# Scan steps traced between single projection tiles, decays split into four steps

## The chip, the core and the metric

The kernel runs on one core of a Trainium2 chip. The metric is the device time of one execution in microseconds (us); the median of three runs of the kernel before is 1252.73 us. Five engines work side by side, each through its own queue of instructions in order: TensorE (PE in the profile; its weight loads are PEld), VectorE (DVE), ScalarE (ACT), GpSimd (POOL) and SyncE (SP), which here only issues transfers.

## The reference, cut to what matters

One layer of a diffusion backbone on 512 latent tokens and 256 context tokens of width 1024. One input projection (`w_in`) feeds a convolution branch and a state-space mixer that scans in both directions; both are gated, merged, projected, and an MLP follows. The change touches the mixer and the convolution branch's first half (GLU and taps):

```python
glu = proj[..., COL_GLU:COL_GATE]
u = glu[..., :CONV_DIM] * jax.nn.sigmoid(glu[..., CONV_DIM:])
u = dwconv(u.reshape(bsz * n_seg, seg_len, CONV_DIM), ...)       # 31 taps
...
xbc = jax.nn.silu(dwconv(proj[..., COL_XBC:COL_DT], ...))        # x, B, C: 5 taps
# the scan, per direction, in chunks of 128 tokens
decay = jnp.exp(jnp.where(lower, seg, -jnp.inf))                 # seg[q,k] = cum[q] - cum[k]
cb = jnp.einsum('bcqgn,bckgn->bcgqk', cs_, bs)
y_diag = jnp.einsum('bcgrqk,bckgrp->bcqgrp', cb[:, :, :, None] * decay, xdt)
states = jnp.einsum('bcqgn,bcqgr,bcqgrp->bcgrpn', bs, decay_to_end, xdt)
y_off = jnp.einsum('bcqgn,bcgrpn,bcqgr->bcqgrp', cs_, h_in, jnp.exp(cum))
y = y_f + flip(y_b) + D * x;  y = rmsnorm(y * silu(z))
```

There are 32 heads in 8 groups of 4; a group shares B and C.

## The kernel before

Activations lie transposed, 128 channels on the partitions and 512 tokens along the row. Every matrix product of a projection is made of three fp32r products (high by high, high by low, low by high). `load_w` (L104) loads a raw weight tile of 128x1024 (two buffers), rounds it on ScalarE to `whi` (L110), and subtracts on VectorE to get `wlo` (L111); `gemm` (L114) then runs 24 matmuls of 512 columns into one of three PSUM buffers `ps`.

The kernel opens with the adaLN modulation and the first projections, then runs the mixer over 8 groups (about 107 to 605 us of the profile), then the rest of the GLU tiles, gates, output projections and the MLP.

A group g needs six projection tiles, made by `proj` (L425): B, C, X0 and X1 through `xbc` (L384), which also does the 5 taps on VectorE (L381) and a SiLU on ScalarE (L391), B and the two X with 256 context columns besides; and Z0, Z1 with a SiLU (L440). The scan of a group is `ssd` (L471):

- `cps` = B by C per chunk (L476), copied to `cb` (L478); transposes of B to `bps` (L484), copied to `Bk` (L485).
- transposes of X to `xps` (L495), scaled on VectorE to `xw` (L500) and copied on ScalarE to `xt` (L507).
- the state of each chunk, `sps` (L515), the first copied on ScalarE to `hst` (L521), the others added up on VectorE (L527, L528).
- for each half j of two heads: four rows of exp(cum) are broadcast from DRAM to `Cd` (L537) and multiplied by C on GpSimd or VectorE (L538); the decays `M` of the two heads are multiplied by `cb` (L541); 32 matmuls with the states (L555) and 16 with `xt` (L551; the profile's counts) fill `yps`; then `yt` (L559, L560), which goes to DRAM, and its square (L566), which GpSimd adds up (L567).

The decays come from `expo` (L450). For each head and each of two directions it broadcasts a row of cum from DRAM to a tile `E` (L459), masks it on GpSimd (L463), takes the exponential on ScalarE in four pieces (L466), and adds the two directions on VectorE (L468). Before the loop it is traced for four heads; then each half y of a group traces the next two heads, all four steps in a row. The forward tiles have 7 buffers, the backward ones 3.

`glu` (L570) makes one of 8 GLU tiles from two projection tiles, with a Tanh (L576) between, and `taps` (L584) its 31-tap convolution on VectorE (30 instructions at L594). Five of the eight are traced inside the group loop, one at the end of groups 0 to 4. The order of tracing per group is thus: whole scan of g, all six projection tiles of g+1, a GLU tile and its taps.

That order is not the order in which engines run. A planner lays out each engine's queue when the kernel is built: an instruction's priority is its place in the tracing, moved by `later(n)`; among those that it takes to be ready at a moment of its own simulated time, the first in priority goes next. Weight loads are moved 300 places ahead (`W_EARLY`), evictions 400 (`EVICT`), taps 650 back (`TAPS_LATER`). What the planner lays out is fixed; on the chip each engine takes its queue in order.

Of the kernel before, what the change touches and what calls it, by code (L numbers as in the profile page):

```python
# [20 lines left out]
G = 8  # L21
# [8 lines left out]
CDB, EB, LEAD, ADDV, E_LATER, E_LATER0 = 7, 7, 2, 1, 0, 0  # L30
# [18 lines left out]
GLU_AT = tuple(range(5))  # L49
# [12 lines left out]
def build(tc, xT, ctxT, cond, crow, wada1, wada2, vecs, hv, cst, w_in, w_co, w_so, w_o, w_1, w_2, outT):  # L62
    nc = tc.nc
    with ExitStack() as es:
# [49 lines left out]
        def gemm(ps, w, rhs, start=True, stop=True, t0=0, t1=None, k0=0, k1=KT):  # L114
            whi, wlo = w
            rhi, rlo = rhs
            ps = ps[:, t0:t1]
            for k in range(k0, k1):
                nc.tensor.matmul(ps, lhsT=whi[:, k, :], rhs=rhi[:, k, t0:t1], start=start and k == 0, stop=False)  # L119
                nc.tensor.matmul(ps, lhsT=whi[:, k, :], rhs=rlo[:, k, t0:t1], start=False, stop=False)  # L120
                nc.tensor.matmul(ps, lhsT=wlo[:, k, :], rhs=rhi[:, k, t0:t1], start=False, stop=stop and k == KT - 1)  # L121

        psum_pools = [pp]
        turn = [0]
# [300 lines left out]
        def proj(g):  # L425
            s = W_GRP + 6 * g
            if g == 0:
                _, Bt, Ct, X = first_xbc
            else:
                Bt = xbc(s, 16 + g, True, "Bt")  # L430
                Ct = xbc(s + 1, 24 + g, False, "Ct")
                X = [xbc(s + 2 + j, 2 * g + j, True, "Xt") for j in range(2)]
            Z = []
            for j in range(2):
# [6 lines left out]
                Z.append(z)  # L441
            return Bt, Ct, X, Z
# [4 lines left out]
        ahead = []  # L447
        asked = [0]

        def expo(upto):  # L450

            while asked[0] < min(upto, HEADS):
                h = asked[0]
                asked[0] += 1
                es_ = []
                for d in range(2):
                    hd = d * HEADS + h
                    e = (tp if d else spool).tile([P, T], F32, name="E", tag="M" if d else "E", bufs=3 if d else EB)
                    nc.sync.dma_start(e, s_cf[hd, 0].unsqueeze(0).broadcast_to([P, T]))  # L459

                    x3 = e.rearrange("p (c q) -> p c q", q=P)
                    sign = -1 if d else 1
                    nc.gpsimd.affine_select(x3, x3, pattern=[[0, NCH], [sign, P]], compare_op=ALU.is_ge,  # L463
                                            fill=never, base=0, channel_multiplier=-sign)
                    for c in range(NCH):
                        nc.scalar.activation(x3[:, c], x3[:, c], AF.Exp, bias=bT[:, c, hd:hd + 1])  # L466
                    es_.append(e)
                (nc.vector if ADDV else nc.gpsimd).tensor_tensor(es_[0], es_[0], es_[1], ALU.add)  # L468
                ahead.append(es_[0])

        def ssd(g, Bt, Ct, X, Z):  # L471
            ch = lambda t, c: t[:, c * P:(c + 1) * P]

            cps = pm.tile([P, T], F32, name="cps", tag="pm")
            for c in range(NCH):
                nc.tensor.matmul(ch(cps, c), lhsT=ch(Bt, c), rhs=ch(Ct, c), start=True, stop=True)  # L476
# [4 lines left out]
            for c0, n in ((0, 4), (4, 2)):  # L481
                pt = pm.tile([P, T], F32, name="bps", tag="pm")
                for c in range(n):
                    nc.tensor.transpose(ch(pt, c), ch(Bt, c0 + c), ident)  # L484
                nc.scalar.copy(Bk[:, c0 * P:(c0 + n) * P], pt[:, :n * P])  # L485

            xt = spool.tile([P, NCH, 4, 64], F32, name="xt", tag="xt", bufs=1)
            xw = [spool.tile([P, 5, 4, 64], F32, name=f"xw{d}", tag=f"xw{d}", bufs=1) for d in range(2)]
            wi = [lambda c: c if c < 3 else c - 1, lambda c: c - 1]
            hs = lambda d: slice(d * HEADS + 4 * g, d * HEADS + 4 * g + 4)  # L490
            for c0 in (4, 0, 2):
                pt = pm.tile([P, T], F32, name="xps", tag="pm")
                for c in range(2):
                    for j in range(2):
                        nc.tensor.transpose(  # L495
                            pt[:, c * 256 + j * P:c * 256 + (j + 1) * P], ch(X[j], c0 + c), ident)
# [5 lines left out]
                for d in range(2):  # L502
                    lo = c0 + 1 if (d == 1 and c0 == 0) else c0
                    hi = c0 + 1 if (d == 0 and c0 == 2) else c0 + 2
                    scaled(xw[d][:, wi[d](lo):wi[d](hi - 1) + 1], ptv[:, lo - c0:hi - c0], wgT[:, lo:hi, hs(d)])
                if c0 < 4:
                    nc.scalar.copy(xt[:, c0:c0 + 2], ptv)  # L507

            hst = spool.tile([P, NCH, 2, 256], F32, name="hst", tag="hst", bufs=1)

            def states(chunks):
                ps = pm.tile([P, T], F32, name="sps", tag="pm")
                for d in range(2):
                    for i, c in enumerate(chunks[d]):
                        nc.tensor.matmul(  # L515
                            ps[:, d * 256:(d + 1) * 256], lhsT=ch(Bk, c),
                            rhs=xw[d][:, wi[d](c)].rearrange("p h e -> p (h e)"),
                            start=i == 0, stop=i == len(chunks[d]) - 1)
# [3 lines left out]
            for s in range(NCH - 1):  # L522
# [5 lines left out]
                nc.vector.tensor_tensor(nxt, nxt, ps.rearrange("p (d h e) -> p d h e", d=2, h=4), ALU.add)  # L528

            for j in range(2):  # L530
                yps = py.tile([P, T], F32, name="yps", tag="py")
                Ms, Cs = [], ([], [])
                for r in range(2):
                    for d in range(2):
                        hd = d * HEADS + 4 * g + 2 * j + r
                        Cd = (spool if d else tp).tile([P, T], F32, name="Cd", tag="Cd", bufs=CDB if d else 3)
                        nc.sync.dma_start(Cd, s_cf[hd, 1].unsqueeze(0).broadcast_to([P, T]))  # L537
                        (nc.vector if (d, r) in DECAYS_V else nc.gpsimd).tensor_tensor(Cd, Ct, Cd, ALU.mult)  # L538
                        Cs[d].append(Cd)
                    M = ahead.pop(0)  # L540
                    nc.vector.tensor_tensor(M, M, cb, ALU.mult)  # L541
                    Ms.append(M)
                with later(E_LATER):
                    expo(4 * g + 2 * j + 2 + LEAD)
                for k in range(3):
                    for c in range(NCH):
                        for r in range(2):
                            o = yps[64 * r:64 * r + 64, c * P:(c + 1) * P]
                            hr = 2 * j + r
                            if k == 2:  # L550
                                nc.tensor.matmul(o, lhsT=xt[:, c, hr, :], rhs=ch(Ms[r], c),  # L551
                                                 start=False, stop=True, skip_group_check=True)
                            else:
                                s = 3 - c if k else c
                                nc.tensor.matmul(o, lhsT=hst[:, s, k, hr * 64:hr * 64 + 64], rhs=ch(Cs[k][r], c),  # L555
                                                 start=k == 0 and c == 0, stop=False, skip_group_check=True)
                t = 2 * g + j
                yt = tp.tile([P, T], F32, name="yt", tag="yt", bufs=2)
                nc.vector.scalar_tensor_tensor(yt, X[j][:, :T], vcol(V_D + t), yps, ALU.mult, ALU.add)  # L559
                nc.vector.tensor_tensor(yt, yt, Z[j], ALU.mult)  # L560
                nc.sync.dma_start(s_y[t], yt)
                if t == 0:
                    nc.scalar.activation(yacc, yt, AF.Square)
                else:
                    q = spool.tile([P, T], F32, name="ysq", tag="ysq", bufs=1)
                    nc.scalar.activation(q, yt, AF.Square)  # L566
                    nc.gpsimd.tensor_tensor(yacc, yacc, q, ALU.add)  # L567


        def glu(t, pool, tag):  # L570
# [4 lines left out]
            with later(-EVICT_GLU):  # L575
                nc.scalar.activation(sg, pb, AF.Tanh, scale=0.5)  # L576
            wa = load_w(w_in[W_GLU + 2 * t + 1])
# [37 lines left out]
        late = list(range(len(GLU_AT), KT))  # L615
# [28 lines left out]
        for t in late:  # L644
            q = glu(t, tp, "e")
# [251 lines left out]
```

## Times and profile before

| | |
|---|---|
| three runs | 1252.73, 1250.56, 1253.77 us (median 1252.73) |
| profiled execution | 1248.84 us, span of the program in it 1247.0 us |
| granted TensorE clock, mean | 0.993 |
| weight tiles through L110 | 163, mean 1049 ns |
| exponentials at L466 | 256 pieces, mean 393 ns |
| masks at L463 | 64, mean 979 ns |
| rows `E` and `Cd` | 64 transfers each of 256 KB, 4.9 and 4.8 us to landing |

The profile is of one execution. A waits view gives an engine's idle time by what ended it: total us, times, longest. A windows view gives each engine's busy time in a stretch, with the number of instructions that touch it. A timeline view gives start and length of merged instructions, and in brackets the idle time before them and what ended it. Ends of matmuls are modelled: back to back, they overlap in the trace, so a busy TensorE isn't one at its full pace. SP's waits for buffers cost nothing by themselves.

### The profile page before, as it was taken

What the parts mean: (1) busy time and instruction counts of PE and PEld (TensorE: products, weight loads), DVE (VectorE), ACT (ScalarE), POOL (GpSimd) and SP (SyncE); (2) the same over time, 40 slices, a digit from 0 to 9 for tenths busy, and PEclk for the clock granted to TensorE, in tenths of its full rate; (3) what the DMA queues carried; (4) which work ended last, traced back from release to release, by engine and by line L of the source; (5) the groups of instructions that cost most, each with busy time, mean ns of one, the idle gap of its engine ahead of it and who ended that gap; (6) DMA issues with size and microseconds to landing.
All of it is one profiled execution on the core that took longest, in us unless ns stands there. A gap on an engine that the chain in (4) does not pass through costs nothing.

```text
span 1247.0 us, 17404 instructions
## 1 busy us (share of the span) xinstructions
PE 1202.9 (96%) x6662; PEld 995.0 (80%) x6662; DVE 924.0 (74%) x1426; ACT 545.2 (44%) x900; POOL 173.4 (14%) x138
## 2 busy tenths in 40 slices
PE   6998999999999999999999999999999999999997
PEld 3787788787787887787888788788988888888886
DVE  6798799899998989776999698776833343443454
ACT  4557876455554445342452561234522332322342
POOL 0004444142242424120010000000000000000000
PEclk8999999999999999999999999999999999999998
DMA  9427573442535352322353468945112323322332
GB/s 366 142 68 225 163 228 103 125 150 93 178 93 178 110 162 78 118 71 91 123 180 119 134 198 289 308 150 166 54 41 96 101 90 97 102 93 94 101 101 68
DMA packets 65331, 169.83 MB, mean 136 GB/s; under 512 B 7648, under 2 KB 10464, under 8 KB 65120
## 3 DMA queue, kind: packets, MB, share of 16 engines
q1 hardware_dynamic: 65248, 168.72, 42.0%
q8 instruction: 52, 0.85, 0.3%
q14 instruction: 31, 0.25, 0.1%
HBM read 162.14 MB, written 6.55 MB: 135 GB/s over the span
## 4 chain that ended last, share of the span: by engine, by line
PE 59%; DVE 21%; DMA 10%; ACT 4%; issue 3%; POOL 1%; SPq 0%; DVEq 0%; ACTq 0%; POOLq 0%
PE ps L119 18%; PE ps L121 18%; PE ps L120 17%; DVE conv L594 7%; DVE wlo L111 3%; PE sps L515 3%; DMA Cd<-s_cf 3%; DVE Xt L381 3%; DMA aw<-in_wada_dram 2%; PE yps L555 1%; DMA E<-s_cf 1%; DVE Ct L381 1%; DMA yr<-s_y 1%; DVE Bt L381 1%; POOL E L463 1%
## 5 line engine op out<-in xcount | busy, mean ns | idle before, releaser
L110 ACT CAST whi<-raw 128x1024 fp32r<-128x1024 f32 x163 | 170.9, 1049 | 363.6 <-PE ps L120 332.5
L111 DVE TENSOR_TENSOR wlo<-raw,whi 128x1024 fp32r<-128x1024 f32 x163 | 203.5, 1249 | 98.3 <-ACT whi L110 86.8
L121 PE MATMUL ps<-hh,wlo 128*128 128x512 f32 x632 | 254.6, 403 | 3.8 <-DVE wlo L111 3.6
L119 PE MATMUL ps<-hh,whi 128*128 128x512 f32 x632 | 255.2, 404 | 2.5 <-DVE Bt L381 1.7
L120 PE MATMUL ps<-hl,whi 128*128 128x512 f32 x632 | 253.7, 401 | 0.0
L594 DVE SCALAR_TENSOR_TENSOR conv<-sg,V,conv 128x392 f32<-128x392 f32 (+14 forms) x240 | 181.7, 774 | 1.8
L121 PEld LDWEIGHTS ps<-hh,wlo 128*128 128x128 f32 x632 | 118.9, 188 | 33.3 <-DVE wlo L111 7.6
L119 PEld LDWEIGHTS ps<-hh,whi 128*128 128x128 f32 x632 | 118.9, 188 | 30.4 <-issue 6.3
L120 PEld LDWEIGHTS ps<-hl,whi 128*128 128x128 f32 x632 | 118.8, 188 | 25.2 <-issue 1.6
L732 DVE SCALAR_TENSOR_TENSOR x<-ps,mod,x 128x512 f32<-128x512 f32 (+1 forms) x48 | 31.7, 661 | 100.5 <-PE ps L121 100.5
L466 ACT ACTIVATE E<-E,bT 128x128 f32<-128x128 f32 x256 | 79.8, 393 | 35.7 <-POOL E L463 35.5
L120 PE MATMUL ps<-h2l,whi 128*128 128x512 f32 (+1 forms) x240 | 89.9, 375 | 0.1
L121 PE MATMUL ps<-h2h,wlo 128*128 128x512 f32 (+1 forms) x240 | 89.8, 375 | 0.0
L119 PE MATMUL ps<-h2h,whi 128*128 128x512 f32 (+1 forms) x240 | 89.4, 375 | 0.0
L120 PE MATMUL ps<-gl,whi 128*128 128x512 f32 x224 | 88.4, 395 | 0.0
L538 POOL TENSOR_TENSOR Cd<-Ct,Cd 128x512 f32<-128x512 f32 x48 | 76.6, 1624 | 84.4 <-ACT Ct L391 70.1
L119 PE MATMUL ps<-gh,whi 128*128 128x512 f32 x224 | 88.2, 394 | 0.0
L121 PE MATMUL ps<-gh,wlo 128*128 128x512 f32 x224 | 87.9, 392 | 0.0
L463 POOL TENSOR_SCALAR_AFFINE_SELECT E<-E 128x512 f32<-128x512 f32 x64 | 61.7, 979 | 182.5 <-DVE Bt L381 100.5
L381 DVE SCALAR_TENSOR_TENSOR Xt<-ps,V,Xt 128x510 f32<-128x510 f32 (+3 forms) x128 | 74.3, 605 | 4.3 <-ACT Xt L377 3.9
L119 PE MATMUL ps<-hc,whi 128*128 128x256 f32 x184 | 52.1, 283 | 1.4 <-DVE Xt L381 1.4
L120 PE MATMUL ps<-hc,whi 128*128 128x256 f32 x184 | 52.2, 284 | 0.0
(260 smaller groups left out, 2282.4 us busy)
## 6 DMA issues: line engine op xcount, KB each, us to landing
raw<-in_w_in_dram SPq DMA_DIRECT2D x81, 512.0 KB, 3.6
raw<-in_w_dram SPq DMA_DIRECT2D x64, 512.0 KB, 3.6
E<-s_cf SPq DMA_DIRECT2D x64, 256.0 KB, 4.9
Cd<-s_cf SPq DMA_DIRECT2D x64, 256.0 KB, 4.8
aw<-in_wada_dram SPq DMA_DIRECT2D x64, 256.0 KB, 4.0
ablk<-in_wada_dram SPq DMA_DIRECT2D x16, 512.0 KB, 9.0
raw<-in_w_so_dram SPq DMA_DIRECT2D x16, 512.0 KB, 3.6
s_y<-yt SPq DMA_DIRECT2D x16, 256.0 KB, 3.3
```

Source lines behind the costliest of these rows:

```text
L110: nc.scalar.copy(hi, raw)
L111: nc.vector.tensor_tensor(lo, raw, hi, ALU.subtract)
L119: nc.tensor.matmul(ps, lhsT=whi[:, k, :], rhs=rhi[:, k, t0:t1], start=start and k == 0, stop=False)
L120: nc.tensor.matmul(ps, lhsT=whi[:, k, :], rhs=rlo[:, k, t0:t1], start=False, stop=False)
L121: nc.tensor.matmul(ps, lhsT=wlo[:, k, :], rhs=rhi[:, k, t0:t1], start=False, stop=stop and k == KT - 1)
L381: nc.vector.scalar_tensor_tensor(o[:, lo:hi], ps[:, lo + d:hi + d], vcol(V_SCW + 5 * ch + j), o[:, lo:hi], ALU.mult, ALU.add)
L463: nc.gpsimd.affine_select(x3, x3, pattern=[[0, NCH], [sign, P]], compare_op=ALU.is_ge, fill=never, base=0, channel_multiplier=-sign)
L466: nc.scalar.activation(x3[:, c], x3[:, c], AF.Exp, bias=bT[:, c, hd:hd + 1])
L515: nc.tensor.matmul(ps[:, d * 256:(d + 1) * 256], lhsT=ch(Bk, c), rhs=xw[d][:, wi[d](c)].rearrange("p h e -> p (h e)"), start=i == 0, stop= ...
L538: (nc.vector if (d, r) in DECAYS_V else nc.gpsimd).tensor_tensor(Cd, Ct, Cd, ALU.mult)
L594: nc.vector.scalar_tensor_tensor(o[:, :, lo:hi], u[:, :, lo + d:hi + d], wv(j), o[:, :, lo:hi], ALU.mult, ALU.add)
L732: nc.vector.scalar_tensor_tensor(x1[:, j, a:b], ps[:, a:b], mod[:, gcol + j, 0:1], x1[:, j, a:b], ALU.mult, ALU.add)
```

## The change

`ssd` is cut into `ssd_c` (cps, cb, Bk), `ssd_x` (xps, xw, xt), `ssd_s` (states) and `ssd_y` (one half), `proj` makes a single tile, `glu` is cut into `glu_b` and `glu_a`, and two strings give the order of tracing. Capitals are projection tiles of the next group; `s`, `y0`, `y1` are of the current group, `c` and `x` of the next (`c0`, `x0` of the first); `e` is one step of the decays, `E` their beginning; `Gb Ga` is a GLU tile, left out once five are made. Group 0 now has two GLU tiles, groups 1 to 3 have one.

The decays of a head are spread over four steps: at step n the rows of head n+5 are loaded, head n+4 is masked, the exponentials of n+3 are taken, and the two directions of n+2 are added. The first of the four exponential pieces of each tile is tied to come after whatever was traced last on ScalarE before it (`keep_in_program_order`: order in ScalarE's queue, no wait). `pe` would tie TensorE's matmuls in the same way, but its flag is never set, so their order stays with the planner. The computation and all buffer counts are the same.

```diff
-CDB, EB, LEAD, ADDV, E_LATER, E_LATER0 = 7, 7, 2, 1, 0, 0
+STEPS0 = 'Gb Ga c0 B x0 C X0 s E e X1 e y0 e Gb Ga y1 e c Z0 Z1 x'
+STEPS = 'B s e C e Gb Ga X0 y0 e X1 e y1 c Z0 Z1 x'
+LEADS = (2, 3, 4, 5)
+CDB, EB = 7, 7
-GLU_AT = tuple(range(5))
+NGLU = 5
...
-        def expo(upto):
-            while asked[0] < min(upto, HEADS):
-                h = asked[0]
...
-                    for c in range(NCH):
-                        nc.scalar.activation(x3[:, c], x3[:, c], AF.Exp, bias=bT[:, c, hd:hd + 1])
-                (nc.vector if ADDV else nc.gpsimd).tensor_tensor(es_[0], es_[0], es_[1], ALU.add)
+        def after_traced(ins):
+            tc.keep_in_program_order(ins)
+        def expo_rows(h):
+            for d in range(2):
+                e = (tp if d else spool).tile([P, T], F32, name="E", tag="M" if d else "E", bufs=3 if d else EB)
+                nc.sync.dma_start(e, s_cf[d * HEADS + h, 0].unsqueeze(0).broadcast_to([P, T]))
+                chain[d][h] = e
...
+        def expo_exp(h):
+            for d in range(2):
+                hd = d * HEADS + h
+                e3 = chain[d][h].rearrange("p (c q) -> p c q", q=P)
+                for c in range(NCH):
+                    i = nc.scalar.activation(e3[:, c], e3[:, c], AF.Exp, bias=bT[:, c, hd:hd + 1])
+                    if c == 0:
+                        after_traced(i)
...
+        def expo_first():
+            for h in range(LEADS[3]):
+                expo_rows(h)
+            for h in range(LEADS[2]):
+                expo_select(h)
+            for h in range(LEADS[1]):
+                expo_exp(h)
+            for h in range(LEADS[0]):
+                expo_add(h)
+        def expo():
+            n = step[0]
+            step[0] += 1
+            for lead, f in zip(LEADS, (expo_add, expo_exp, expo_select, expo_rows)):
+                if 0 <= n + lead < HEADS:
+                    f(n + lead)
...
-        cur = proj(0)
-        with later(E_LATER0):
-            expo(2 + LEAD)
+        cur = group(0)
+        proj(cur, "Z0")
+        proj(cur, "Z1")
         for g in range(G):
-            ssd(g, *cur)
-            if g + 1 < G:
-                cur = proj(g + 1)
-            if g in GLU_AT:
-                with later(GLU_LATER):
-                    q = glu(GLU_AT.index(g), spool, "sg")
-                with later(TAPS_LATER):
-                    taps(*q)
+            nxt = group(g + 1)
+            for part in STEPS0.split() if g == 0 else STEPS.split():
+                in_order[0] = False
...
+                elif part == "e":
+                    expo()
...
+                elif part == "Gb":
+                    if begun_glu < NGLU:
+                        glu_q = glu_b(begun_glu, spool, "sg")
+                        begun_glu += 1
+                elif glu_q is not None:
+                    glu_q = glu_a(*glu_q)
+                    with later(TAPS_LATER):
+                        taps(*glu_q)
+                    glu_q = None
+            cur = nxt
```

More of the change, by code (lines that the diff above doesn't have):

```diff
@@ L118, in gemm, with pe @@
             for k in range(k0, k1):
-                nc.tensor.matmul(ps, lhsT=whi[:, k, :], rhs=rhi[:, k, t0:t1], start=start and k == 0, stop=False)
-                nc.tensor.matmul(ps, lhsT=whi[:, k, :], rhs=rlo[:, k, t0:t1], start=False, stop=False)
-                nc.tensor.matmul(ps, lhsT=wlo[:, k, :], rhs=rhi[:, k, t0:t1], start=False, stop=stop and k == KT - 1)
+                pe(nc.tensor.matmul(ps, lhsT=whi[:, k, :], rhs=rhi[:, k, t0:t1], start=start and k == 0, stop=False))
+                pe(nc.tensor.matmul(ps, lhsT=whi[:, k, :], rhs=rlo[:, k, t0:t1], start=False, stop=False))
+                pe(nc.tensor.matmul(ps, lhsT=wlo[:, k, :], rhs=rhi[:, k, t0:t1], start=False, stop=stop and k == KT - 1))
         psum_pools = [pp]
+        in_order = [False]
+        def pe(ins):
+            if in_order[0]:
+                tc.keep_in_program_order(ins)
         turn = [0]
@@ L423, in build, with group, proj @@
         never = nc.gpsimd.to_reg(NEVER)
-        def proj(g):
-            s = W_GRP + 6 * g
+        def group(g):
             if g == 0:
                 _, Bt, Ct, X = first_xbc
-            else:
[L430 to L434, printed above, removed]
+                return {"g": 0, "B": Bt, "C": Ct, "X0": X[0], "X1": X[1]}
+            return {"g": g}
+        def proj(q, part):
+            g = q["g"]
+            s = W_GRP + 6 * g
+            j = int(part[1:] or 0)
+            if part == "B":
+                q[part] = xbc(s, 16 + g, True, "Bt")
+            elif part == "C":
+                q[part] = xbc(s + 1, 24 + g, False, "Ct")
+            elif part[0] == "X":
+                q[part] = xbc(s + 2 + j, 2 * g + j, True, "Xt")
+            else:
                 w = load_w(w_in[s + 4 + j], early=W_EARLY if g else 0)
@@ L440, in proj @@
                     nc.scalar.activation(z, ps, AF.Silu)
-                Z.append(z)
-            return Bt, Ct, X, Z
+                q[part] = z
         def bc(ap, shape):
             return ap.unsqueeze(len(shape) - 1).broadcast_to(shape)
-        ahead = []
-        asked = [0]
-        def expo(upto):
-            while asked[0] < min(upto, HEADS):
-                h = asked[0]
[L454 to L464, printed above, removed]
-                    for c in range(NCH):
-                        nc.scalar.activation(x3[:, c], x3[:, c], AF.Exp, bias=bT[:, c, hd:hd + 1])
-                    es_.append(e)
-                (nc.vector if ADDV else nc.gpsimd).tensor_tensor(es_[0], es_[0], es_[1], ALU.add)
-                ahead.append(es_[0])
@@ L471, in ssd @@
-        def ssd(g, Bt, Ct, X, Z):
-            ch = lambda t, c: t[:, c * P:(c + 1) * P]
+        chain = [[None] * HEADS for _ in range(2)]
+        step = [0]
+        def after_traced(ins):
+            tc.keep_in_program_order(ins)
+        def expo_rows(h):
[3 more added lines that the diff above has]
+                chain[d][h] = e
@@ new lines, in expo_select @@
+        def expo_select(h):
+            for d in range(2):
+                e3 = chain[d][h].rearrange("p (c q) -> p c q", q=P)
+                sign = -1 if d else 1
+                nc.gpsimd.affine_select(e3, e3, pattern=[[0, NCH], [sign, P]], compare_op=ALU.is_ge,
+                                        fill=never, base=0, channel_multiplier=-sign)
+        def expo_exp(h):
+            for d in range(2):
+                hd = d * HEADS + h
+                e3 = chain[d][h].rearrange("p (c q) -> p c q", q=P)
+                for c in range(NCH):
+                    i = nc.scalar.activation(e3[:, c], e3[:, c], AF.Exp, bias=bT[:, c, hd:hd + 1])
+                    if c == 0:
+                        after_traced(i)
@@ new lines, in expo_add @@
+        def expo_add(h):
+            f, b = chain[0][h], chain[1][h]
+            nc.vector.tensor_tensor(f, f, b, ALU.add)
+        def expo_first():
[13 more added lines that the diff above has]
+                    f(n + lead)
@@ L474, in ssd, with hs, ssd_c @@
+        ch = lambda t, c: t[:, c * P:(c + 1) * P]
+        wi = [lambda c: c if c < 3 else c - 1, lambda c: c - 1]
+        def hs(g, d):
+            return slice(d * HEADS + 4 * g, d * HEADS + 4 * g + 4)
+        def ssd_c(q):
+            Bt, Ct = q["B"], q["C"]
             cps = pm.tile([P, T], F32, name="cps", tag="pm")
             for c in range(NCH):
-                nc.tensor.matmul(ch(cps, c), lhsT=ch(Bt, c), rhs=ch(Ct, c), start=True, stop=True)
+                pe(nc.tensor.matmul(ch(cps, c), lhsT=ch(Bt, c), rhs=ch(Ct, c), start=True, stop=True))
@@ L514, in states @@
                     for i, c in enumerate(chunks[d]):
-                        nc.tensor.matmul(
+                        pe(nc.tensor.matmul(
                             ps[:, d * 256:(d + 1) * 256], lhsT=ch(Bk, c),
                             rhs=xw[d][:, wi[d](c)].rearrange("p h e -> p (h e)"),
-                            start=i == 0, stop=i == len(chunks[d]) - 1)
+                            start=i == 0, stop=i == len(chunks[d]) - 1))
                 return ps
@@ L528, in ssd @@
                 nc.vector.tensor_tensor(nxt, nxt, ps.rearrange("p (d h e) -> p d h e", d=2, h=4), ALU.add)
[L530 to L567, printed above, removed]
@@ L570, in glu, with ssd_y @@
-        def glu(t, pool, tag):
+            q["hst"] = hst
+        def ssd_y(q, j):
+            g, Ct, cb, xt, hst, X, Z = q["g"], q["C"], q["cb"], q["xt"], q["hst"], q[f"X{j}"], q[f"Z{j}"]
+            yps = py.tile([P, T], F32, name="yps", tag="py")
+            Ms, Cs = [], ([], [])
+            for r in range(2):
+                for d in range(2):
+                    hd = d * HEADS + 4 * g + 2 * j + r
+                    Cd = (spool if d else tp).tile([P, T], F32, name="Cd", tag="Cd", bufs=CDB if d else 3)
+                    nc.sync.dma_start(Cd, s_cf[hd, 1].unsqueeze(0).broadcast_to([P, T]))
+                    (nc.vector if (d, r) in DECAYS_V else nc.gpsimd).tensor_tensor(Cd, Ct, Cd, ALU.mult)
+                    Cs[d].append(Cd)
+                M = chain[0][4 * g + 2 * j + r]
+                nc.vector.tensor_tensor(M, M, cb, ALU.mult)
+                Ms.append(M)
+            for k in range(3):
+                for c in range(NCH):
+                    for r in range(2):
+                        o = yps[64 * r:64 * r + 64, c * P:(c + 1) * P]
+                        hr = 2 * j + r
+                        if k == 2:
+                            pe(nc.tensor.matmul(o, lhsT=xt[:, c, hr, :], rhs=ch(Ms[r], c),
+                                             start=False, stop=True, skip_group_check=True))
+                        else:
+                            s = 3 - c if k else c
+                            pe(nc.tensor.matmul(o, lhsT=hst[:, s, k, hr * 64:hr * 64 + 64], rhs=ch(Cs[k][r], c),
+                                             start=k == 0 and c == 0, stop=False, skip_group_check=True))
+            t = 2 * g + j
+            yt = tp.tile([P, T], F32, name="yt", tag="yt", bufs=2)
+            nc.vector.scalar_tensor_tensor(yt, X[:, :T], vcol(V_D + t), yps, ALU.mult, ALU.add)
+            nc.vector.tensor_tensor(yt, yt, Z, ALU.mult)
+            nc.sync.dma_start(s_y[t], yt)
+            if t == 0:
+                nc.scalar.activation(yacc, yt, AF.Square)
+            else:
+                y2 = spool.tile([P, T], F32, name="ysq", tag="ysq", bufs=1)
+                nc.scalar.activation(y2, yt, AF.Square)
+                nc.gpsimd.tensor_tensor(yacc, yacc, y2, ALU.add)
@@ L571, in glu, with glu_b @@
+        def glu_b(t, pool, tag):
             wb = load_w(w_in[W_GLU + 2 * t])
@@ L576, in glu, with glu_a @@
                 nc.scalar.activation(sg, pb, AF.Tanh, scale=0.5)
+            return t, sg
+        def glu_a(t, sg):
             wa = load_w(w_in[W_GLU + 2 * t + 1])
@@ L644, in build @@
         for t in late:
[L645 removed]
+            q = glu_a(*glu_b(t, tp, "e"))
             with later(LATE_LATER):
```

35 lines of the change are left out of this document (28 added, 7 removed).

## The prediction

> **What bounds the kernel now.** I read the page's busy times first, then the windows of the stretch that the change touches, then what TensorE waits for there, and last the chain and the timeline at the longest of these waits.
>
> ```profile
> span 1247.0 us, 17404 instructions
> PE 1202.9 (96%) x6662; PEld 995.0 (80%) x6662; DVE 924.0 (74%) x1426; ACT 545.2 (44%) x900; POOL 173.4 (14%) x138
> ```
>
> TensorE is the bound: 96% of the span, and no other engine is near it on average. The group loop lies between 107 and 605 us. The windows give span, PE, PEld, DVE, ACT and POOL busy there: the whole loop, its start, its middle, its end, one group with a GLU tile, one without; and two single gemms of 24 matmuls, 512 and 256 columns wide.
>
> ```profile
> 107.00:605.00 498.00, 479.36 (x2942) 398.24 (x2941) 443.72 (x631) 256.06 (x501) 159.54 (x124) 1.00 0.43 134
> 107.00:160.00 53.00, 46.62 (x303) 37.91 (x302) 41.80 (x54) 43.23 (x90) 28.84 (x25) 0.97 0.68 208
> 160.00:465.00 305.00, 296.03 (x1833) 247.14 (x1832) 288.27 (x411) 157.90 (x324) 100.95 (x79) 1.00 0.44 139
> 465.00:605.00 140.00, 136.71 (x810) 113.19 (x809) 113.64 (x168) 54.92 (x90) 29.75 (x21) 1.00 0.30 95
> 242.00:310.84 68.84, 67.07 (x407) 55.83 (x406) 65.04 (x93) 33.84 (x66) 22.72 (x17) 1.00 0.41 131
> 509.20:566.00 56.80, 55.84 (x359) 47.18 (x358) 41.46 (x61) 22.29 (x33) 13.54 (x10) 1.00 0.29 93
> 202.86:208.31 5.45, 5.45 (x26) 4.51 (x25) 5.45 (x9) 1.68 (x3) 5.09 (x4) 1.00 0.01 3
> 199.98:202.86 2.88, 2.88 (x26) 2.87 (x25) 2.88 (x5) 1.13 (x2) 0.00 (x0) 1.00 0.26 104
> ```
>
> TensorE is idle for 498.00 - 479.36 = 18.6 us in the loop, 6.4 of them in its first 53 us. No matmul is added or taken away, so this idle time is nearly all that an order of tracing can win. VectorE is the runner-up: 65.0 of 68.8 us in a group with a GLU tile, 41.5 of 56.8 in one without. What ends the idle time (total, times, longest):
>
> ```profile
> PE yps L555 <- DVE Cd L538: 5.2, 8, 1.4
> PE sps L515 <- ACT xt L507: 4.3, 1, 4.3
> PE ps L121 <- DVE wlo L111: 3.6, 5, 0.7
> PE xps L495 <- ACT Bk L485: 2.3, 4, 1.2
> PE ps L119 <- DVE Bt L381: 1.2, 4, 0.4
> PE xps L495 <- ACT cb L478: 0.7, 1, 0.7
> PE sps L515 <- DVE xw L500: 0.6, 1, 0.6
> PE ps L119 <- DVE Ct L381: 0.5, 1, 0.5
> ```
>
> These add up to 18.4 us in 25 waits, the 18.6 of the windows. None names `E`: the decays cost TensorE nothing directly. They cost it through ScalarE's queue, whose own waits and timeline show how:
>
> ```profile
> ACT E L466 <- POOL E L463: 35.5, 17, 4.4
> ...
> 117.31 2.44 ACT L466 ACTIVATE E<-E,bT 128x128 f32<-128x128 f32 x8
> 124.19 1.28 ACT L466 ACTIVATE E<-E,bT 128x128 f32<-128x128 f32 x4 [4.44 <-POOL E L463]
> 125.37 1.04 ACT L507 COPY xt<-xps 128x512 f32<-128x512 f32 x2
> 126.32 0.59 ACT L521 COPY hst<-sps 128x512 f32<-128x512 f32 x1
> ```
>
> From 119.75 to 124.19 ScalarE stands at an exponential whose mask GpSimd hasn't made. The copies of `xt` stand behind it in the queue, and TensorE stands at a state product behind them: the 4.3 us wait.
>
> **The change, part by part.**
>
> *First group: exponentials behind the state copy.* `E` is now traced after `s`, and each tile's first exponential is tied behind what ScalarE was given last, the copy to `hst`. The copies of `xt` were given before that, so the queue can't hold these exponentials ahead of them: the 4.3 us go. (Three of a tile's four pieces are untied, but they need the mask too, and masks and rows are traced one and two steps earlier.) With `xw` and `cb` a tile or more away from who needs them, the 0.6 and 0.7 go as well: -5.6. Next late would be y0 of group 0, which needs four tiles of exponentials: two bursts of 2.44, 4.9 us, plus the additions. X1 stands between, 5.45 + 2.88 = 8.3 us of TensorE. Without that cover some 5 us come back; I take nothing.
>
> *Cd between the halves.* Before, y1 follows y0 by a few matmuls of the next group. The chain shows why it waits:
>
> ```profile
> 380.08 1.06 PE yps L555 x16
> 381.14 0.03 issue
> 381.17 3.20 DMA Cd<-s_cf
> 384.37 0.03 issue
> 384.40 0.02 DVEq L538
> 384.42 0.04 issue
> 384.46 0.69 DVE Cd L538
> ```
>
> The buffers of `Cd` come free with y0's matmuls; then row, product, y1: 5.1 us from 380.08 to 385.15. With X1 and two decay steps traced between y0 and y1, 8.3 us of gemm stand there, with 3.2 to spare. The last group has no X1, so about one wait of 5.2 / 8 = 0.65 stays: -4.5. The rows of `E`, loads through SP's queue too, now ask for one head at a time, two rows rather than four; a `Cd` row behind them waits less, if anything. I take nothing.
>
> *Transposes of X.* The 2.3 us are `xps` waiting for a bank that `Bk`'s copy should have freed, a copy that stands behind exponentials on ScalarE. Now Z0 and Z1 (two gemms, 10.9 us) are traced between `c` and `x`: -2.3.
>
> *Weights.* The 3.6 us on `wlo` and 1.7 on the evictions of B and C stay: a saturated VectorE puts them there, and no VectorE instruction is gone. What the change adds is on ScalarE. Exponentials and SiLUs don't share a table here:
>
> ```profile
> L466 ACT ACTIVATE E<-E,bT 128x128 f32<-128x128 f32 x256 | 79.8, 393 | 35.7 <-POOL E L463 35.5
> L110 ACT CAST whi<-raw 128x1024 fp32r<-128x1024 f32 x56 | 58.4, 1043 | 87.1 <-PE ps L120 70.7 <-issue 16.0 <-ACT E L466 0.3
> ...
> L466 ACT ACT_TABLE_LOAD x10 | 12.8, 1283 | 4.4 <-DMA E<-s_cf 4.3
> ...
> L391 ACT ACT_TABLE_LOAD x8 | 10.3, 1283 | 3.1 <-DVE Bt L381 2.9
> ```
>
> Now a group has four bursts of exponentials, each after the SiLU of another tile (B, C, X0 with y0, X1): up to eight table loads instead of the two or three of 18 in seven groups. Six more at 1.28 in seven groups are 54 us of ScalarE; 498.0 - 256.1 = 242 are free, so it won't be the bound. But the next weight's rounding can stand behind a burst. That rounding may start when the gemm before last is through, and it and the subtraction
>
> ```profile
> L111 DVE TENSOR_TENSOR wlo<-raw,whi 128x1024 fp32r<-128x1024 f32 x163 | 203.5, 1249 | 98.3 <-ACT whi L110 86.8
> ```
>
> take 1.04 + 1.25 = 2.3 of a 5.45 us gemm: slack 3.15. A table load and eight exponentials are 1.28 + 2.44 = 3.7: 0.57 too late if it meets the rounding squarely. Bounds: nothing (the bursts fall between roundings), or four hits a group at the 0.7 of the longest wait for `wlo`, 28 x 0.7 = 20. I take one a group, +4.0 for seven, because bursts of eight stand in the queue now too, as in the timeline above, and the weights cost only five waits. By the Trainium skill, page "ScalarE: Activation LUTs", section "What ACT_TABLE_LOAD costs", a switch is about 2.66 us with its drain; the trace shows 1.28 for the load and can't show the drain. By the page's figure a burst would be 1.95 late, and the sum 9.7 us worse.
>
> *GLU earlier.* The second GLU tile in group 0 brings VectorE work forward:
>
> ```profile
> L594 DVE SCALAR_TENSOR_TENSOR conv<-sg,V,conv 128x392 f32<-128x392 f32 (+11 forms) x175 | 139.5, 802 | 1.5
> ```
>
> 30 taps of 0.80 are 24 us, with two `wlo` 26.5, against 10.9 of TensorE. The loop's start has 53.0 - 41.8 = 11.2 us of VectorE idle. Taps are 650 places back, so I take zero; the bounds are below, as a rival.
>
> *Sum.* -5.6 - 4.5 - 2.3 + 4.0 = -8.4. After the loop nothing is changed, TensorE is busy from there on, and the gain carries to the end. The profiled execution took 1248.84 us, so 1240.4 on its own measure; the median of the runs, 1252.73, is 3.9 above it, so **1244 us** for a median.
>
> **Rivals.** A measurement of this kernel tells 0.3% (3.8 us) from no change.
>
> - *All idle time goes.* Tracing in the order in which things are wanted also frees the banks earlier, and the weights' waits go. 1252.7 - 18.6 = 1234; since a matmul is shown 404 ns long at a pace of 5.45 / 24 = 227, each of 25 waits hides up to 0.17 more: 1230. The row for the 404:
>
> ```profile
> L119 PE MATMUL ps<-hh,whi 128*128 128x512 f32 x632 | 255.2, 404 | 2.5 <-DVE Bt L381 1.7 <-DVE Ct L381 0.5
> ```
>
>  Against: VectorE at 94% of the GLU groups makes `wlo` late whatever the tracing.
> - *The waits move.* TensorE's order is still the planner's, whose arrivals miss the chip's by half a microsecond or so; two or three such waits a group come back elsewhere. 1249 to 1256. For it: the waits are short and recur in each group alike.
> - *VectorE sets the pace to the end of group 3.* If the taps brought forward stand ahead of subtractions, 26.5 - 11.2 - 10.9 = 4.4 us of work are over, with no slack to recover in, while TensorE's gains there win nothing: about +2, 1255. Against: the 650 places.
> - *Slower: table loads and bursts in front of the roundings.* If two of the four bursts of a group meet a rounding, with a load on either side (1.28 + 2.44 + 1.28 = 5.0 against the slack of 3.15), each costs 1.85: 2 x 7 x 1.85 = 26 instead of 4, so 1252.7 - 12.4 + 26 = 1266. It ends slower from about 16 us of such waits on, nine hits in 28 bursts. For it: four tied bursts among five SiLUs leave the planner no way to batch them. Against: ScalarE is free half the time. The same page of the Trainium skill, "Table sets: the hidden batching unit", says to batch calls by table set, which this change undoes; the trace's two or three loads a group agree that the order before batched them.
>
> **How the numbers follow.** Forecast (1240 to 1249) 0.42; all idle time goes 0.18; the waits move 0.12; VectorE's pace 0.08; slower through ScalarE 0.20. So faster 0.60, same 0.20, slower 0.20. The range runs from 1230 to 1262: the lower end is the second case, the upper takes half of the last; a tenth or so is left out above and a twentieth below.
>
> **What would show it.** In the profile after: the 4.3 us wait for `xt` gone, waits for masks on ScalarE well under 35.5, `yps` on `Cd` about 1, `xps` on `Bk` near nothing, table loads on the two lines above from 18 to some 40 to 60, waits of TensorE on `wlo` around 8, idle time of TensorE in the loop about 10 instead of 18.6. Idle time near 18 with other names would be the moved waits; waits on `wlo` above 16 the rival on ScalarE; VectorE above 97% from 107 to 400 us together with them, VectorE's pace.

## The result, and the profile after

The changed kernel takes 1263.1 us as median of four runs (1261.0 to 1264.1) against 1251.6 before on the same chip: a ratio of 1.0088, 95% interval 1.0067 to 1.0109. It is slower by 11.5 us, where a gain of 8.4 us was forecast. The profiled execution took 1264.1, span 1262.3. First the page's busy times, then windows of the group loop (from the first `cps` to the sum over `yacc`: whole, start, GLU groups, rest).

```profile
span 1262.3 us, 17441 instructions
PE 1205.4 (95%) x6662; PEld 1005.1 (80%) x6662; DVE 926.4 (73%) x1426; ACT 626.2 (50%) x962; POOL 167.6 (13%) x138
```

```profile
100.80:619.70 518.90, 487.40 (x2979) 413.31 (x2978) 452.28 (x641) 341.35 (x566) 159.12 (x131) 0.97 0.42 131
100.80:160.00 59.20, 45.94 (x259) 38.45 (x258) 40.76 (x61) 39.65 (x83) 23.78 (x23) 0.86 0.46 148
160.00:420.00 260.00, 244.26 (x1454) 207.50 (x1453) 255.52 (x359) 171.51 (x280) 79.63 (x62) 0.97 0.42 130
420.00:619.70 199.70, 197.20 (x1270) 167.35 (x1269) 156.01 (x224) 130.19 (x203) 55.71 (x46) 1.00 0.41 127
```

TensorE runs the same 6662 matmuls and is idle 56.9 us of the span instead of 44.1; with 2.5 more of busy time that is the whole 15.3 by which the span grew. All of it lies in the loop, which has 31.5 us of idle time against 18.6: 13.3 in its start, 15.7 up to 420 us, and only 2.5 in the groups after that. The granted clock (third from the end) fell too, to 0.86 at the start; what that costs sits inside the busy time. ScalarE is busy 81 us more with 62 more instructions: table loads, on these lines in the loop (before, 10, 8 and 2), of 1.28 us each.

```profile
L491 ACT ACT_TABLE_LOAD x42 | 53.9, 1283 | 13.1 <-DMA E<-s_cf 12.5
L402 ACT ACT_TABLE_LOAD x28 | 35.9, 1283 | 39.7 <-DVE Bt L392 27.7 <-DVE Xt L392 7.7 <-DVE Ct L392 4.1
L460 ACT ACT_TABLE_LOAD x13 | 16.7, 1283 | 0.2
```

What TensorE waits for in the loop now:

```profile
PE sps L573 <- ACT hst L579: 10.8, 4, 4.6
PE ps L124 <- DVE Bt L392: 8.4, 1, 8.4
PE ps L126 <- DVE wlo L116: 8.0, 7, 2.8
PE ps L124 <- DVE Xt L392: 2.4, 1, 2.4
PE sps L573 <- DVE xw L554: 0.8, 1, 0.8
PE ps L124 <- ACT whi L115: 0.6, 2, 0.4
PE yps L614 <- DVE Cd L599: 0.4, 1, 0.4
```

The waits on `Cd` (5.2 before, 0.4 now) and of `xps` (3.0) are gone as forecast. In their place stand four waits for the copy of the first states to `hst`, one of 8.4 us for the first B to leave its bank, and twice the time on `wlo`. Fewer waits than before, but long ones. ScalarE's own waits say what is in the way; then its timeline ahead of TensorE's two longest waits, start and length with the idle time before in brackets:

```profile
ACT E L491 <- POOL E L483: 51.1, 20, 7.3
ACT L491 <- DMA E<-s_cf: 12.5, 6, 9.2
...
112.63 1.28 ACT L491 ACT_TABLE_LOAD   x1 [9.19 <-DMA E<-s_cf]
...
117.47 0.76 ACT L388 ACTIVATE Bt<-ps,V 128x512 f32<-128x512 f32 x1
...
139.28 1.28 ACT L491 ACTIVATE E<-E,bT 128x128 f32<-128x128 f32 x4 [3.73 <-POOL E L483]
140.57 1.28 ACT L402 ACT_TABLE_LOAD   x1
141.87 0.63 ACT L402 ACTIVATE Ct<-Ct 128x512 f32<-128x512 f32 x1
142.40 0.55 ACT L388 ACTIVATE Xt<-ps,V 128x256 f32<-128x256 f32 x1
142.85 1.03 ACT L115 CAST whi<-raw 128x1024 fp32r<-128x1024 f32 x1
143.79 0.58 ACT L579 COPY hst<-sps 128x512 f32<-128x512 f32 x1
```

The eviction of B at 117.47 and the copy to `hst` at 143.79 both come behind exponentials that waited for rows or masks, 9.2 and 3.7 us. Five more pieces stand between that eviction and the one of B's context columns at 121.32, and VectorE's taps on B only end after that. At 139.28 four pieces of exponentials run ahead of the copy behind which only the first piece of a tile is tied. Before, ScalarE waited 35.5 us for masks; now 51.1, and 12.5 for rows.

### The profile page after: what moved, and what is told of

Read it like the earlier page. It is cut to its first block, busy times and chain, and to the rows that moved or that the text cites. A ratio compares the mean times of both kernels' runs of the same rounds, so it can differ in the third digit from the quotient of the medians.

```text
span 1262.3 us, 17441 instructions
## 1 busy us (share of the span) xinstructions
PE 1205.4 (95%) x6662; PEld 1005.1 (80%) x6662; DVE 926.4 (73%) x1426; ACT 626.2 (50%) x962; POOL 167.6 (13%) x138
## 4 chain that ended last, share of the span: by engine, by line
PE 63%; DVE 17%; DMA 9%; ACT 6%; issue 4%; POOL 1%; SPq 0%; DVEq 0%; ACTq 0%; POOLq 0%
PE ps L124 19%; PE ps L126 19%; PE ps L125 19%; DVE conv L656 5%; DVE wlo L116 3%; DMA E<-s_cf 3%; DMA aw<-in_wada_dram 2%; DVE Xt L392 2%; PE sps L573 2%; PE yps L614 1%; ACT whi L115 1%; DMA yr<-s_y 1%; DMA raw<-in_w_dram 1%; ACT E L491 1%; DVE xw L554 1%
## 5 line engine op out<-in xcount | busy, mean ns | idle before, releaser
L116 DVE TENSOR_TENSOR wlo<-raw,whi 128x1024 fp32r<-128x1024 f32 x163 | 202.7, 1244 | 96.4 <-ACT whi L115 88.9
L126 PE MATMUL ps<-hh,wlo 128*128 128x512 f32 x632 | 251.4, 398 | 8.8 <-DVE wlo L116 8.8
L125 PE MATMUL ps<-hl,whi 128*128 128x512 f32 x632 | 249.7, 395 | 0.0
L656 DVE SCALAR_TENSOR_TENSOR conv<-sg,V,conv 128x472 f32<-128x472 f32 (+14 forms) x240 | 178.0, 767 | 3.7 <-ACT conv L650 1.4
L491 ACT ACTIVATE E<-E,bT 128x128 f32<-128x128 f32 x256 | 85.9, 394 | 51.6 <-POOL E L483 51.1
L483 POOL TENSOR_SCALAR_AFFINE_SELECT E<-E 128x512 f32<-128x512 f32 x64 | 58.6, 927 | 293.2 <-DMA E<-s_cf 228.3
L392 DVE SCALAR_TENSOR_TENSOR Xt<-ps,V,Xt 128x510 f32<-128x510 f32 (+3 forms) x128 | 74.7, 607 | 15.3 <-ACT Xt L388 14.8
L599 POOL TENSOR_TENSOR Cd<-Ct,Cd 128x512 f32<-128x512 f32 x48 | 71.4, 1505 | 69.3 <-ACT Ct L402 37.1
L491 ACT ACT_TABLE_LOAD x42 | 53.9, 1283 | 13.1 <-DMA E<-s_cf 12.5
L124 PE MATMUL ps<-hc,whi 128*128 128x256 f32 x184 | 52.8, 287 | 3.9 <-DVE Xt L392 3.9
```

What stands on the lines that cost most here:

```text
L116: nc.vector.tensor_tensor(lo, raw, hi, ALU.subtract)
L124: pe(nc.tensor.matmul(ps, lhsT=whi[:, k, :], rhs=rhi[:, k, t0:t1], start=start and k == 0, stop=False))
L125: pe(nc.tensor.matmul(ps, lhsT=whi[:, k, :], rhs=rlo[:, k, t0:t1], start=False, stop=False))
L126: pe(nc.tensor.matmul(ps, lhsT=wlo[:, k, :], rhs=rhi[:, k, t0:t1], start=False, stop=stop and k == KT - 1))
L392: nc.vector.scalar_tensor_tensor(o[:, lo:hi], ps[:, lo + d:hi + d], vcol(V_SCW + 5 * ch + j), o[:, lo:hi], ALU.mult, ALU.add)
L483: nc.gpsimd.affine_select(e3, e3, pattern=[[0, NCH], [sign, P]], compare_op=ALU.is_ge, fill=never, base=0, channel_multiplier=-sign)
```

## The experiments

Three theories at first. *Masks*: three of four pieces aren't tied, the planner lays them out as soon as it takes their masks to be ready, and on the chip the masks come later. *Switching*: the table loads, 83 in the loop instead of 20. *VectorE*: the second GLU tile in group 0. Each run is told as a ratio to runs of the kernel before on the same chip, with its 95% interval, and its median.

**The tie.** No tie at all, and every piece tied:

```diff
                     i = nc.scalar.activation(e3[:, c], e3[:, c], AF.Exp, bias=bT[:, c, hd:hd + 1])
-                    if c == 0:
-                        after_traced(i)        # e1: both lines go
+                    after_traced(i)            # e2: for every c
```

> The changed kernel without the tie of the exponentials. Three theories. Switching: ScalarE loads a table 83 times in the group loop instead of 20, 81 us more, and what stands behind a load or a burst (evictions, roundings, the copy to hst) reaches TensorE late. Masks: ScalarE stands at exponentials laid out ahead of their masks (51 us of waits for masks, 12.5 for rows), and evictions stand behind them. VectorE: the second GLU tile in group 0 keeps VectorE full from 107 to 420 us. This layout has 21 table loads fewer than the changed kernel. Switching expects a third of the loss back, about 1259; masks expects no gain or a loss, 1263 to 1270, as nothing holds the exponentials; VectorE expects 1263.

> The changed kernel with all four pieces of an exponential tied behind what was traced before, not the first alone. Masks expects the waits of ScalarE for masks to fall under 15 us, the waits of TensorE for the hst copy (10.8) and for the first B (8.4) to go, and about 1250. Switching: 13 table loads fewer only, about 1261. VectorE: 1263.

No tie: 1.0118 (1.0095 to 1.0142), 1262.5 us, the intervals with the changed kernel overlapping: the tie of one piece in four does nothing that can be measured. It has 62 table loads in the loop, 21 fewer, and isn't faster, against switching. But it speaks against masks in its first form too: ScalarE waits only 14.4 us for masks and 14.3 for rows here, less than half, with no gain. Its timeline ahead of a wait of 4.3 us for the copy to `hst` shows more:

```profile
404.58 0.99 ACT L491 ACTIVATE E<-E,bT 128x128 f32<-128x128 f32 x3
405.46 0.77 ACT L388 ACTIVATE Bt<-ps,V 128x512 f32<-128x512 f32 x1
406.13 2.15 ACT L491 ACTIVATE E<-E,bT 128x128 f32<-128x128 f32 x7
408.17 0.56 ACT L388 ACTIVATE Bt<-ps,V 128x256 f32<-128x256 f32 x1
408.62 1.05 ACT L115 CAST whi<-raw 128x1024 fp32r<-128x1024 f32 x1
410.50 0.40 ACT L491 ACTIVATE E<-E,bT 128x128 f32<-128x128 f32 x1 [0.83 <-POOL E L483]
410.81 0.56 ACT L577 COPY hst<-sps 128x512 f32<-128x512 f32 x1
```

Free exponentials are slipped in between the evictions and ahead of the copy, eleven of them here; most run rather than wait. So the theory becomes: free pieces stand ahead of what TensorE needs, whether they wait for masks, run, or load a table. All tied: **0.9965 (0.9947 to 0.9984), 1245.1 us**, faster than the kernel before, and 1.2% below the changed kernel by the condition of one line. Its windows, what TensorE waits for, and ScalarE's waits in the loop, longest first; no wait for a mask or a row is among ScalarE's any more:

```profile
100.30:600.90 500.60, 481.77 (x2978) 412.14 (x2977) 446.11 (x640) 323.92 (x553) 158.07 (x131) 0.98 0.44 136
...
PE sps L572 <- ACT hst L578: 10.4, 2, 6.8
PE yps L613 <- DVE Cd L598: 4.5, 3, 2.1
PE ps L126 <- DVE wlo L116: 3.5, 3, 1.4
PE ps L124 <- DVE Xt L392: 0.2, 1, 0.2
...
ACT L402 <- DVE Xt L392: 42.3, 11, 10.5
ACT whi L115 <- PE ps L125: 30.9, 13, 4.3
ACT Ct L402 <- DVE Ct L392: 27.8, 6, 9.8
```

That the free pieces do it is borne out; switching alone isn't, since 70 table loads are still there (on the three lines; 83 in the changed kernel). But not every wait went that masks had named. The one on B is gone (8.4 us), 4.5 us on `wlo` and 2.2 on X with it, and 4.1 us on `Cd` have come back. `hst` stays at 10.4 us in two waits. At the longer, of 6.8 us, the copy now stands behind a SiLU that waits for VectorE's taps; at the other, of 3.6 us, it still stands behind exponentials, tied ones.

```profile
131.36 0.63 ACT L402 ACTIVATE Ct<-Ct 128x512 f32<-128x512 f32 x1 [9.77 <-DVE Ct L392]
...
133.28 0.58 ACT L578 COPY hst<-sps 128x512 f32<-128x512 f32 x1
```

TensorE's idle time in the loop is thus 18.8 us, against 31.5 in the changed kernel and 18.6 in the kernel before.

**The two halves of the change.** e3 keeps the new order of tracing with the old decays (two heads at a time, all four steps in a row, inside each half, no tie); e4 keeps the old order with the new decays:

```diff
# e3, in the new order                          
-                M = chain[0][4 * g + 2 * j + r]
+                M = ahead.pop(0)
...
+            expo(4 * g + 2 * j + 2 + LEAD)     # "e" does nothing
# e4, in the old order
-                with later(E_LATER):
-                    expo(4 * g + 2 * j + 2 + LEAD)
+                expo()
+                expo()
```

> New order of tracing, decays as before: two heads at a time inside each half, all four steps in a row, no tie. It tells the decays from the order of the scan. Masks: the decays' split is what put exponentials ahead of their masks, so near the kernel before, 1250 to 1254. Switching: 21 loads fewer, 41 more than before, about 1259. VectorE: 1263, as the GLU tiles stand as in the changed kernel.

> The other half: the old order of tracing (whole scan, six projection tiles, GLU) with the decays in four steps a head apart and tied. Its table loads are as many as before. Switching: 1252, as before. Masks: slower than before, 1257 or more, with long waits for masks in the first group. VectorE: 1252.

e3: 1.0108 (1.0088 to 1.0127), 1263.1 us. e4: 1.0079 (1.0057 to 1.0101), 1258.9 us. Either half alone costs about as much as both. In e3 TensorE waits 12.4 us for `hst`, in five waits. In e4 there are 20 table loads, as before, and it is slow all the same, which switching can't explain, and masks can. It had put the long waits in the first group, though; most lie later, 47.5 of the 58.2 us between 160 and 465 us. ScalarE's wait for masks and TensorE's longest wait there:

```profile
ACT E L472 <- POOL E L464: 58.2, 24, 5.2
...
PE ps L119 <- DVE Bt L381: 9.5, 5, 2.2
```

Masks was wrong on e3, though: it took the split of the decays for the cause. Free exponentials lose in the new order however they are traced.

**Table loads.** In e5 and e6 the SiLU of B, C, X and Z becomes a Tanh, in the changed kernel and in the kernel before:

```diff
-            nc.scalar.activation(o, o, AF.Silu)
+            nc.scalar.activation(o, o, AF.Tanh)
```

> The changed kernel with the SiLU of B, C, X and Z computed as a Tanh, which uses the same table as the exponentials, so that no table is loaded in the group loop (the SiLU is left out: the output is another). To be held against the same edit in the kernel before. Switching: the loss against that one goes, the two within 3 us, and this one at 1250 or less. Masks or VectorE: this one stays 8 us or more above the other.

> The kernel before with the same edit (SiLU of B, C, X and Z as a Tanh, so no table loads in the loop; the SiLU is left out). Switching: 20 loads less, 1.28 each, mostly hidden: 1247 to 1251. Masks and VectorE: the same, within 3 us of 1251.6.

e5: 1.0051 (1.0031 to 1.0070), 1254.5 us; e6: 1.0019 (1.0004 to 1.0035), 1252.3. The gap shrinks from 11.5 to 2.3 us between the medians, from 0.88% to 0.32% by the ratios, as switching had it; the 1250 or less that it gave for e5 doesn't come, and the kernel before isn't faster without its loads. ScalarE's waits for masks in e5 are 78.8 us, more than in the changed kernel, at a smaller loss. Both kernels also got another layout, so this pair can't tell the loads' cost from the layout's. e12 takes the loads from the all-tied kernel:

> Changed kernel, every exponential tied, and the SiLU of B, C, X and Z as a Tanh (the SiLU is left out), so that no table is loaded in the loop. Told against the all-tied kernel (0.9965 of before, 70 table loads in the loop). If the loads cost by themselves, 60 or more of them at 1.28 us reach TensorE in part: 0.992 or less. If they cost only behind exponentials that wait for masks, 0.995 to 0.998.

0.9981 (0.9967 to 0.9995), against 0.9965 with 70 loads: nothing is won, and it lies just above what was expected (0.995 to 0.998) for loads that cost only behind waiting exponentials. So in the all-tied kernel no cost of the loads can be seen, though this layout too is another. That each free exponential in the changed kernel costs more by the loads around it is a reading that fits e5, not one that was shown.

**The second GLU tile.** One in each of groups 0 to 4, with one piece in four tied (e7), and with all tied (e11):

```diff
-STEPS0 = 'Gb Ga c0 B x0 C X0 s E e X1 e y0 e Gb Ga y1 e c Z0 Z1 x'
+STEPS0 = 'Gb Ga c0 B x0 C X0 s E e X1 e y0 e y1 e c Z0 Z1 x'
```

> The changed kernel without the second GLU tile in group 0: one in each of groups 0 to 4, as before. VectorE: groups 1 to 3 lose their backlog, waits for wlo fall, about 1255. Switching and masks: 1261 to 1265.

> Changed kernel, every exponential tied, and one GLU tile in group 0 rather than two. With one in four tied, one GLU tile took 1257.6 and two took 1263.1. If VectorE's backlog costs by itself, 1240 to 1242 here against 1245.1; if it only added to the waits behind exponentials, 1245.

e7: 1.0063 (1.0038 to 1.0087), 1257.6 us; e11: **0.9924 (0.9898 to 0.9950), 1241.2 us**. They lie 0.25% and 0.41% below their twins with two tiles. The intervals of the first pair overlap, those of the second just touch; together they speak for a cost of some 3 to 5 us. e7 lies between what VectorE (1255) and the others (1261) had; e11 is in the range given for a backlog of VectorE that costs by itself.

**Tie and lead.** What does the tie need in order to pay? The kernel before with all pieces tied (e8); the new order with old decays, all tied (e9); the old order with the four steps, all tied (e10):

```diff
-                        nc.scalar.activation(x3[:, c], x3[:, c], AF.Exp, bias=bT[:, c, hd:hd + 1])
+                        tc.keep_in_program_order(nc.scalar.activation(x3[:, c], x3[:, c], AF.Exp, bias=bT[:, c, hd:hd + 1]))
```

> The kernel before with every exponential tied behind what ScalarE was given before it; nothing else. With all pieces tied the changed kernel takes 1245.1 where it takes 1263.1 with one in four. Two readings. Tie alone: what the exponentials held up goes in any order; in the kernel before 7.3 us of TensorE's waits (xt, Bk, cb) stand behind exponentials, so 1241 to 1244. Tie with lead: here the rows are asked for only two heads ahead and the exponentials are traced right behind their masks, so tied ones still meet masks that aren't there or come late: 1248 or more.

> New order of tracing, decays two heads at a time as before (rows, masks, exponentials traced in a row), every exponential tied. Tie alone: 1245, as with the four steps. Tie with lead: tied exponentials stand in the queue with their masks just traced, ScalarE waits for masks 30 us or more, 1255 or more.

> Old order of tracing, decays in four steps a head apart, every exponential tied. Told against 1258.9 with one in four tied. Either reading expects the waits for masks (58.2) under 15 us. If the gain of the all-tied kernel comes from tie and lead, 1245 here too; if the steps between the tiles bring a part (Cd between the halves, transposes), 1249 or so, with those waits still there.

In this table, the kernels with the new order have two GLU tiles in group 0, those with the old order one:

| decays, order of tracing | free, or one in four tied | all tied |
|---|---|---|
| two heads in a row, old | 1 (the kernel before) | 1.0028 (1.0011 to 1.0045) |
| two heads in a row, new | 1.0108 | 1.0016 (1.0005 to 1.0028) |
| four steps, old | 1.0079 | 0.9967 (0.9949 to 0.9986) |
| four steps, new | 1.0088 (the change) | 0.9965 (0.9947 to 0.9984) |

The medians of the three are 1255.3, 1253.4 and 1246.3 us: e8 came out as tie with lead had it, e9 and e10 each between their two forecasts. Tied without lead, in the new order, exponentials no longer hold up others but come late themselves. That takes back most of the loss (1.0108 to 1.0016), and no more. In e9 TensorE waits for the decay product, which stood in no list before (DVE `E` at L575):

```profile
PE yps L584 <- DVE E L575: 12.3, 5, 4.8
```

I had expected ScalarE to wait 30 us for masks there; it waits for none, and the loss shows up one step further on. In e8 the waits on `Bk` and `cb` went, but the 4.3 us on `xt` stay: in the old order the first exponentials are traced ahead of that copy. What "lead" is made of wasn't told apart: the four steps ask for rows earlier and also set masks and exponentials a step apart, and no run has one without the other.

Tied with lead, both orders of tracing seem to take the same time in the table. But e2 has the second GLU tile in group 0 and e10 hasn't. With one GLU tile in each of groups 0 to 4 on both sides, e11 is to be held against e10, on the same chip: 0.9924 (0.9898 to 0.9950) against 0.9967 (0.9949 to 0.9986), 1241.2 against 1246.3 us, with all four executions of e11 (up to 1241.5) below all ten of e10 (from 1244.2). So the steps between the tiles, the larger part of the diff, do bring some 5 us, which the second GLU tile hid. The waits on `Cd` agree, e10 first:

```profile
PE yps L581 <- DVE Cd L564: 7.9, 8, 1.5
PE yps L613 <- DVE Cd L598: 0.9, 2, 0.6
```

Which of the steps brings how much, and whether the place of a GLU tile within its group has a part in it, wasn't run.

**A version to beat both.** All tied, one GLU tile, and the states of group 0 traced before its C:

```diff
+STEPS0 = 'Gb Ga c0 x0 B s E C e X0 X1 e y0 e y1 e c Z0 Z1 x'
```

> A version to beat both: every exponential tied, one GLU tile in group 0, and the states of group 0 traced before its projection of C (Gb Ga c0 x0 B s E C e X0 X1 e y0 e y1 e c Z0 Z1 x), so that the copy to hst isn't behind the SiLU of C. In the all-tied kernel with one GLU tile the wait for that copy is 4.3 us idle and some 1.5 at a lower clock after it: 1236 if it goes, 1241 if another wait takes its place.

0.9919 (0.9895 to 0.9943), 1237.8 us: faster than both kernels and than the tied old order (e10), and not to be told from e11. The wait for the `hst` copy is gone, and another of its size has taken its place:

```profile
PE ps L124 <- DVE Ct L392: 4.4, 1, 4.4
```

## Why the prediction was wrong

The step that failed is the first of the sum, the exponentials behind the state copy (-5.6), with its parenthesis: three of a tile's four pieces are untied, but they need the mask too. Needing the mask doesn't keep an instruction out of a queue; it makes it wait there with everything behind it. The wait on `xt` did go (4.3), but the untied pieces stood ahead of the first B (8.4 us) and of the copy to `hst` (4.6 of its 10.8). Instead of a gain of 8.4 us, TensorE's idle time in the loop grew by 12.9.

e2 shows that it was these pieces, and e10 against e4 shows the same in the old order (1.0079 to 0.9967). The changed kernel with all of them tied has the sign that was forecast and, at 1245.1, nearly the number (1244). That nearness is luck. The ratio, 0.9965, is half of the forecast gain, because that chip ran the kernel before in 1249.3; and the idle time in the loop, 18.8 us under other names, is not the forecast 10 but what was named as the sign of the moved waits.

- *Cd between the halves*: right, 0.4 us left where 0.65 was said. With all pieces tied, 4.5 us stand there again in e2 and 0.9 in e11.
- *Transposes*: right, none left.
- *Weights*: +4.0 forecast, +4.4 measured (`wlo` 3.6 to 8.0), but not shown to be for the reason given. Table loads on the two lines went from 18 to 70, above the 40 to 60 named; yet e5, with a single load in the loop, still waits 7.3 us on `wlo`, e2, with 70, only 3.5, and e7, with one GLU tile in group 0, 5.7. And the trace can show whether a load costs more than its 1.28 us, which the prediction denied: the load at 140.57 starts 0.01 us after the exponentials before it end, and the SiLU 0.02 us after the load ends, so nothing beside the 1.28 is seen.
- *GLU earlier*: taken at zero; e7 and e11 put it at some 3 to 5 us, around the upper bound of 4.4. Its rival's sign was only in part there: VectorE was busy 93% from 107 to 400 us, not above 97%, but 98% from 160 us on.
- *What no term held*: each long wait costs more than its idle time, by TensorE's clock (below). TensorE's busy time as a whole rose by only 2.5 us of the 15.3 by which the span grew, though; the rest is idle time.
- *The slower rival* had the sign, the engine and nearly the time (1266), but not the wait. Its own test was waits on `wlo` above 16 us; there were 8.0. The place was evictions and copies behind free exponentials, a wait that the prediction had found in the trace of before and believed cured.
- *Moved waits* at "half a microsecond or so" missed by size: at the start of the loop, where a chain of transfers, masks and exponentials begins, ScalarE stood 9.2 us at one row.

Open is how the loss divides between exponentials that wait, those that run, and the table loads around them; e1 shows that waiting isn't all of it, and e5 leaves the loads a possible part.

## What to carry to other kernels

Work that is ready early fills a queue ahead of work that others wait for, so hold back all pieces of a group, not the first, and give them enough lead that holding them back doesn't make them late. Here the tie alone took back most of the new order's loss, and cost 0.3% in the old order; only with lead did either order come out below the kernel before. When waits are read for what a change will cure, ask of each instruction that stays free where it can now go. A change in several parts is best run with each part alone, and compared with everything else equal: here the condition of one line decided the sign, and a GLU tile moved forward hid what the large part was worth.

## What the runs showed of the hardware

TensorE's granted clock falls after an idle stretch, and the next matmuls pay. Windows of the changed kernel (span, busy times, and third from the end the clock): the 4.6 us wait, the two stretches of 4 us after it, and a stretch at full clock for comparison; then a wait of 2.4 us and the 4 us after it; then one of 1.7 and what came after that.

```profile
139.80:144.40 4.60, 0.00 (x0) 0.00 (x0) 2.65 (x5) 4.55 (x9) 1.85 (x3) 0.92 0.00 0
144.40:148.40 4.00, 3.98 (x9) 3.17 (x10) 4.00 (x6) 3.81 (x10) 2.89 (x2) 0.50 0.32 74
148.40:152.40 4.00, 4.00 (x15) 3.17 (x14) 4.00 (x8) 3.73 (x4) 0.00 (x0) 0.74 0.33 125
210.40:214.40 4.00, 4.00 (x19) 3.34 (x18) 3.15 (x5) 2.67 (x6) 1.20 (x1) 1.00 0.00 0
378.90:381.90 3.00, 0.56 (x4) 0.17 (x2) 3.00 (x4) 0.00 (x0) 1.08 (x1) 1.00 0.00 0
381.90:384.00 2.10, 2.10 (x12) 2.10 (x13) 2.10 (x5) 0.20 (x1) 0.00 (x0) 0.66 0.61 232
384.00:386.00 2.00, 2.00 (x11) 2.00 (x11) 2.00 (x4) 1.49 (x3) 1.43 (x2) 0.50 0.92 304
330.30:332.40 2.10, 0.38 (x3) 0.03 (x1) 2.10 (x4) 2.07 (x3) 0.30 (x1) 1.00 0.29 92
332.40:336.00 3.60, 3.60 (x16) 2.99 (x17) 3.46 (x5) 3.57 (x7) 0.41 (x1) 1.00 0.48 150
```

At 0.50 for 4 us and 0.74 for four more, a wait of 4.6 us costs 2.0 + 1.0 = 3.0 us besides itself. The Trainium skill has this on its page "TensorE: Matmul & The Clock Gate", section "Why this matters for your kernels", which asks for no idle gaps over some 3 us. The trace agrees on the half clock, and shows it after 2.4 us already; the wait of 1.7 us left the clock at 1.00. By these windows, many short waits, as before, are cheaper than a few long ones of the same sum.
